# A hybrid trunk on one core: when the first block's mean square is finished, and which projections run on unnormed channels

## The chip, the cores and the metric

The kernel runs on one core of a Trainium2 chip. The engines of a core are TensorE (PE, matrix products; PEld is its weight load), VectorE (DVE), ScalarE (ACT), GpSimd (POOL) and SyncE (SP, which here issues nearly all transfers, one after another, on a queue of its own). Matrix products leave their sums in PSUM; everything else lies in SBUF or in device memory. The metric is the device time of one execution in microseconds (us).

## The reference, cut to what matters

One layer of a streaming encoder: 2048 tokens, 1024 channels. The first half is an RMS norm, one combined projection, three token mixers that read columns of it, and an output projection; the second half is a gated convolutional network.

```
def rms_norm(x, g):
    xf = x.astype(jnp.float32)
    y = xf * lax.rsqrt(jnp.mean(xf * xf, axis=-1, keepdims=True) + RMS_EPS)
    return (y * g.astype(jnp.float32)).astype(x.dtype)
...
def rwkv7_time_mix(u, mu, w0, w2, a0, a2, g2, k_k, k_a, r_k, lnx_g, lnx_b):
...
    u = u + (u_prev - u) * mu
    r, k, v, w_lo, a_lo, g_lo = jnp.split(u, C_SPLITS, axis=-1)
    w = w0 + jnp.tanh(w_lo) @ w2
```

The mixers are A (chunked softmax attention), B (forgetting attention), both with RMS-normed queries and keys per head of 64 channels, and C (an RWKV-7 recurrence). The factor 1/rms of a token is one number for all its 1024 channels, so a projection of the unnormed channels (times the gain g) may be multiplied by that factor afterwards.

## The kernel before, in words

Tokens are worked on in four blocks of 512. Channels lie on the 128 partitions, so that x of a block is 8 tiles of 128 x 512. Products are made in a split form: a value is a high part `hi` and a rest `lo`, and `project` adds hi·hi, hi·lo and lo·hi for each of the 8 tiles, 24 matmuls in all (L281 to L283). The normalised tiles are called hT. The weights of a projection come by `load_w`: a raw load of 0.5 MB on SP's queue (L270, tile `wraw`, two buffers), a cast of the high part on ACT (L160), the subtraction of the low part on DVE (L161), and a store of the split 1 MB for the later blocks (L273, `wD`).

`prepare` makes the factor: squares of the 8 tiles on ACT (L325), their sum on POOL and DVE (L327, L329), a product with ones on PE (L332), Ln and Exp on ACT (L336, L337, result `rsb`), and the normalisation of x on DVE (L341). `block_in` casts the normalised tiles into hT (L160, L161). In the first block two projections (j12 and j13, the inputs of the decay, the learning rate and the gate) take unnormed tiles `hR`, and their sums are multiplied by `rsb` afterwards (L370). The pool of hT and hR has one buffer for each tile, so a normalised tile is written where the unnormed one was read.

```
    hR = [hTp.tile([P, 2, TB], F32R, name=f"hT{kt}") for kt in range(KT)]
...
    weave((), lora_in(hR, lo0, scale))
    for b in range(NB):
        hT = block_in(xs)
```

`qk_in` makes a query or key tile q0 to q7: a projection, its square on ACT (L700), a product with a block matrix on PE (L703), Ln and Exp (L705, L706), a multiplication (L708), a split into `qh` and `ql`, and two stores on SP (L712, L713). In the first block the projections named in `PRE` come first, then k, r and v of the recurrent mixer in `rwkv_front` (L294 to L300 mix a token with the one before it; L394 and L395 are four small products, whose sigmoid is `sigw`, L305; L423 to L447 prepare the chunks; L467 is the first product of the chunks). `rwkv_back` is the recurrence over chunks: PE adds to `z` (L658, L659), and ACT and DVE make the next state S from it (L662, L663).

The order of instructions on each engine is made when the program is built, by a scheduler that goes by priorities: a priority is the place in the written order, and `tc.high_priority(offset=200)` puts what stands in it 200 places ahead. `weave` and `pipelined` interleave jobs by their count of matmuls; `pipelined` parks a job that yields 0 until `PARK` = 3 tiles of the next projection are through.

Of the kernel before, what the change touches and what calls it, by code (L numbers as in the profile page):

```python
# [33 lines left out]
PACE = 1  # L34
KSTAT = 1
X0N = 1
PRE = "q0 q1"
PLAN0 = ["", "q2 q3 q7", "q4 q6 q5 v1", "v0"]
PLAN = ["q1 v0", "q2 q3", "q4 q5 v1", "q6 q0 q7"]
LAST = ["", "", "v0", "q2 q0", "q1 q6 q3", "q4 v1 q5 q7"]  # L40
# [56 lines left out]
def trunk_kernel(ctx: ExitStack, tc: tile.TileContext, xT, w_in, pp, cst, cau, rel, relr, w2, a2, g2, w_out, w_up, w_down, out, dbg=None):  # L97
    nc = tc.nc
# [80 lines left out]
    def t512(name, tag, dt=F32):  # L179
        return (flp if tag == "fl" else t2k).tile([P, TB], dt, name=name, tag=tag, bufs=BUFS[tag])  # L180
# [74 lines left out]

    kept = {}

    def pair(n):
        return wl.tile([P, 2, n, 1040 // n], F32R, name="w", tag="w", bufs=BUFS["w"])

# [15 lines left out]
    def project(hT, c0, raw=None, who="P"):  # L276

        hi, lo = load_w(0, c0, P, KT, raw)
        ps = psm[who].tile([P, TB], F32, name="mm", tag="ps")
        for kt in range(KT):  # L280
            mm(ps, hi[:, kt, 0:P], hT[kt][:, 0, :], start=(kt == 0), stop=False)  # L281
            mm(ps, hi[:, kt, 0:P], hT[kt][:, 1, :], start=False, stop=False)  # L282
            mm(ps, lo[:, kt, 0:P], hT[kt][:, 0, :], start=False, stop=(kt == KT - 1))  # L283
            yield 3
        return ps
# [23 lines left out]
    def prepare(b, xs, rsbs=None):  # L309

        acc = t512("acc", "fl")

        def load(kt):
            if b == 0:
                return x0[kt]
            xt = xtp.tile([P, TB], F32, name="xt", bufs=BUFS["xt"])
            nc.sync.dma_start(out=xt, in_=xT[kt * P : (kt + 1) * P, b * TB : (b + 1) * TB])
            return xt

        accs = [acc, t512("acc", "fl")] if b == 0 else [acc]  # L320
        n = KT // len(accs)
        for kt in range(KT):
            a, first = accs[kt // n], kt % n == 0
            sq = a if first else t512("sq", "fl")
            nc.scalar.activation(sq, load(kt), AF.Square)  # L325
            if not first:
                (nc.vector if kt // n else LEV["acc"](nc)).tensor_tensor(a, a, sq, op=ALU.add)  # L327
        if b == 0:
            nc.vector.tensor_tensor(acc, acc, accs[1], op=ALU.add)  # L329
        yield 12  # L330
        ps = psm["S"].tile([P, TB], F32, name="mm", tag="ps")
        mm(ps, cn("ones"), acc, start=True, stop=True)  # L332
        rsb = xtp.tile([P, TB], F32, name="rsb")
        if rsbs is not None:
            rsbs.append(rsb)
        nc.scalar.activation(rsb, ps, AF.Ln, scale=1.0 / DM, bias=eps[:, 0:1])  # L336
        nc.scalar.activation(rsb, rsb, AF.Exp, scale=-0.5)  # L337

        def normed(kt):
            xt = load(kt)  # L340
            nc.vector.scalar_tensor_tensor(xt, xt, par("mix_g", kt), rsb, op0=ALU.mult, op1=ALU.mult)  # L341
            return xt

        n = BUFS["xt"] if b else KT
        xs.extend([normed(kt) for kt in range(n)] + [functools.partial(normed, kt) for kt in range(n, KT)])
# [12 lines left out]
    def lora_in(hT, res, scale=None):  # L358
        pss = []
        for j in (12, 13):  # L360
            pss.append((yield from project(hT, CB + j * P, raw0 if scale and j == 12 else None)))
            if scale is None:
                lora_out(j, pss[-1], res)
        if scale is not None:
            rsb = scale()

            def scaled():
                for j in (12, 13):
                    t = t512("t", "fl")
                    nc.vector.tensor_tensor(t, pss[j - 12], rsb, op=ALU.mult)  # L370
                    lora_out(j, t, res)

            late.append(scaled)
# [193 lines left out]
            rows = slice(c * 64, c * 64 + 32)  # L567
            copy(e, DT[rows, :, c * 64 + 32 : c * 64 + 64], ps[rows].rearrange("p w s i -> p (w s) i"))

    def urgent():  # L570
        return tc.high_priority(offset=200)

    def rwkv_back(s):

        b, i, lg, KR, DT, LZ, v, bD, EC = (s[n] for n in ("b", "i", "lg", "KR", "DT", "LZ", "v", "bD", "EC"))
# [116 lines left out]
        nc.vector.tensor_tensor(yl, yl, gps, op=ALU.mult)  # L692
        nc.gpsimd.dma_start(out=yD[512 + i * P : 512 + (i + 1) * P, b * TB : (b + 1) * TB], in_=yl)

    def qk_in(b, hT, n):

        ts_ = slice(b * TB, (b + 1) * TB)
        ps = yield from project(hT, (0, 128, 256, 384, 768, 896, 1024, 1152)[n], None, "Q")
        sq = t512("sq", "fl")
        nc.scalar.activation(sq, ps, AF.Square)  # L700
        yield 0
        sps = psm["q"].tile([P, TB], F32, name="mm", tag="ps")
        mm(sps, cn("blk"), sq, start=True, stop=True)  # L703
        rn = t512("rn", "fl")
        nc.scalar.activation(rn, sps, AF.Ln, scale=1.0 / 64, bias=eps[:, 0:1])  # L705
        nc.scalar.activation(rn, rn, AF.Exp, scale=-0.5)  # L706
        g = qkg[:, n // 2 : n // 2 + 1]
        nc.vector.scalar_tensor_tensor(rn, ps, g, rn, op0=ALU.mult, op1=ALU.mult)  # L708
        qh = t512("qh", "fl", F32R)
        ql = t512("ql", "fl", F32R)  # L710
        split(qh, ql, rn, None, LEV['ql'](nc))
        nc.sync.dma_start(out=qkD[n, 0, :, ts_], in_=f(qh))  # L712
        nc.sync.dma_start(out=qkD[n, 1, :, ts_], in_=f(ql))  # L713
# [54 lines left out]
        nc.sync.dma_start(out=ckD[:, 0, ts_], in_=f(ch))  # L768
        nc.sync.dma_start(out=ckD[:, 1, ts_], in_=f(cl))

    def pipelined(jobs):

        parked = None
        for job in jobs:
            k = 0
            for w in job:
                if w == 0:
                    if parked is not None:
                        yield from parked
                    parked = job  # L780
                    break
                yield w
                k += 1
                if parked is not None and k == PARK:
                    yield from parked
                    parked = None
        if parked is not None:
            yield from parked
# [33 lines left out]
        for _ in stream:  # L822
            pass

    def fill(b, hT, names):
        return pipelined([v_in(b, hT, int(n[1])) if n[0] == "v" else qk_in(b, hT, int(n[1])) for n in names.split()])

    plan, last = PLAN, LAST
    def bias_rows():
# [27 lines left out]
    def scale():  # L857
        for _ in prep:
            pass
        return rsb0[0]  # L860

    weave((), lora_in(hR, lo0, scale))
    for b in range(NB):
        hT = block_in(xs)
        xs = []
        jobs = (PLAN0 if b == 0 else plan) if b + 1 < NB else last
        lo = {} if b else lo0
        for i in range(4):
            res = {}
            if b == 0 and i == 0:  # L870
                late.pop()()
                weave((), fill(b, hT, PRE))
            fills[:] = [fill(b, hT, jobs[i])]
            weave(
                (back, inv),
                lora_in(hT, lo) if i == 0 and b else (),
                rwkv_front(b, i, hT, lo, res),
                prepare(b + 1, xs) if i == 2 and b + 1 < NB else (),
                fills[0],
            )  # L880
            back, inv = (rwkv_back(prev) if prev else None), rwkv_inverse(res)
            prev = res
            if b == 1 and i == 1:
                bias_rows()
            if b == 2 and i == 0:
                bias(0, nc.sync)
# [593 lines left out]
```

## Time and profile before

| | us |
|---|---|
| median of three runs | 3197.59 |
| lowest and highest of them | 3186.72, 3198.84 |
| the profiled execution, its own time | 3200.97 |
| its span | 3199.2 |
| PE busy | 3007.5 |

The rows further down are of that execution. Times are counted from the start of its span. A timeline's row says when an instruction (or a group of equal ones, x2) started, how long it took, the engine, the line and the tile, and in brackets how long the engine had been idle and what ended that. A matmul's length is modelled, so the step from one to the next says more than the length shown. The mean granted clock of PE over the span was 0.967 of full speed.

### The profile page before, as it was taken

To read this page: it belongs to the slowest core of one execution; us is meant where nothing else is said; L and a number is where in the kernel's file an instruction comes from. 1 tells how busy PE (TensorE), PEld (TensorE's weight loads), DVE (VectorE), ACT (ScalarE), POOL (GpSimd) and SP (SyncE) were. 2 spreads that over 40 slices of the span, in tenths; PEclk is the share of its full clock that TensorE was granted. 3 is DMA by queue.
4 is the path that set the end of the run, shared out by engine and by line. 5 is a ranking of instruction groups with operands and counts; after the bars stand their busy time and mean duration, and the time that the engine had idled before them with its cause. 6 is when DMAs were issued, how large, how long until landed. Compare 5 with 4: busy or idle time off the path is not lost.

```text
span 3199.2 us, 49138 instructions
## 1 busy us (share of the span) xinstructions
PE 3007.5 (94%) x17820; PEld 2634.3 (82%) x17820; DVE 2366.6 (74%) x4590; ACT 1398.1 (44%) x2610; POOL 955.5 (30%) x928
## 2 busy tenths in 40 slices
PE   6988999999999989999989899998999998999999
PEld 4666777777777756667789899998999998899998
DVE  6667676756777646777462888889988888888886
ACT  5444444544443335678532433434333434333332
POOL 1010010001001021144241444444444445444443
PEclk8988999999999979999999999999999999999999
DMA  7756665655644475423234322222422222422221
GB/s 223 210 166 182 194 176 150 175 158 166 187 122 128 134 177 152 132 77 94 67 118 133 132 80 80 80 79 79 147 80 80 80 80 84 136 75 76 80 80 68
DMA packets 310818, 392.92 MB, mean 123 GB/s; under 512 B 137144, under 2 KB 228804, under 8 KB 299752
## 3 DMA queue, kind: packets, MB, share of 16 engines
q1 hardware_dynamic: 305936, 378.44, 40.3%
q0 software_dynamic: 2816, 8.39, 0.9%
q10 hardware_dynamic: 1824, 2.95, 0.4%
q8 instruction: 141, 2.31, 0.3%
q14 instruction: 101, 0.83, 0.1%
HBM read 304.65 MB, written 86.36 MB: 122 GB/s over the span
## 4 chain that ended last, share of the span: by engine, by line
PE 66%; DVE 17%; DMA 5%; issue 5%; ACT 4%; POOL 2%; SPq 1%; POOLq 0%; ACTq 0%; DVEq 0%
PE ps L1307 7%; PE ps L1306 7%; PE ps L1305 7%; PE ps L1351 4%; PE ps L1353 4%; PE ps L1352 4%; PE mm L283 2%; PE mm L281 2%; PE mm L282 2%; PE o L1077 2%; PE z L658 2%; DVE T L536 2%; DVE tm L533 2%; PE ps L1213 2%; DVE wu L161 2%
## 5 line engine op out<-in xcount | busy, mean ns | idle before, releaser
L1307 PE MATMUL ps<-B,wu 128*128 128x340 f32 (+1 forms) x1848 | 593.9, 321 | 19.7 <-DVE wu L161 19.6
L1305 PE MATMUL ps<-B,wu 128*128 128x340 f32 (+1 forms) x1848 | 590.1, 319 | 3.0 <-ACT wu L160 2.1
L1306 PE MATMUL ps<-B,wu 128*128 128x340 f32 (+1 forms) x1848 | 590.7, 320 | 0.0
L1307 PEld LDWEIGHTS ps<-B,wu 128*128 128x128 f32 x1848 | 349.1, 189 | 26.8 <-DVE wu L161 26.4
L1351 PE MATMUL ps<-hid,wd 128*128 128x340 f32 (+1 forms) x1056 | 341.2, 323 | 13.9 <-ACT wd L160 10.3
L1305 PEld LDWEIGHTS ps<-B,wu 128*128 128x128 f32 x1848 | 349.0, 189 | 3.6 <-ACT wu L160 2.4
L1306 PEld LDWEIGHTS ps<-B,wu 128*128 128x128 f32 x1848 | 348.2, 188 | 0.1
L1353 PE MATMUL ps<-hid,wd 128*128 128x340 f32 (+1 forms) x1056 | 337.2, 320 | 4.5 <-POOL wd L161 4.5
L1352 PE MATMUL ps<-hid,wd 128*128 128x340 f32 (+1 forms) x1056 | 339.0, 321 | 0.0
L281 PE MATMUL mm<-hT,w 128*128 128x512 f32 x704 | 314.6, 447 | 20.8 <-ACT w L160 13.6
L161 DVE TENSOR_TENSOR wu<-S,wu 128x512 fp32r<-128x512 f32 x264 | 255.9, 976 | 74.9 <-ACT wu L160 74.9
L282 PE MATMUL mm<-hT,w 128*128 128x512 f32 x704 | 289.3, 411 | 6.8 <-DVE hT L161 6.1
L283 PE MATMUL mm<-hT,w 128*128 128x512 f32 x704 | 289.6, 411 | 1.9 <-DVE w L161 1.8
L1354 DVE TENSOR_TENSOR acc<-acc,ps 128x340 f32<-128x340 f32 (+1 forms) x528 | 247.4, 503 | 48.8 <-PE ps L1353 48.7
L161 POOL TENSOR_TENSOR wd<-raw,wd 128x1024 fp32r<-128x1024 f32 x66 | 171.7, 2621 | 271.5 <-ACT wd L160 271.4
L160 ACT CAST wu<-S 128x512 fp32r<-128x512 f32 x264 | 162.9, 618 | 150.3 <-PE ps L1307 144.1
L1351 PEld LDWEIGHTS ps<-hid,wd 128*128 128x128 f32 x1056 | 200.8, 190 | 17.3 <-ACT wd L160 11.1
L161 DVE TENSOR_TENSOR wu<-raw,wu 128x512 fp32r<-128x512 f32 x198 | 202.6, 1024 | 5.5 <-ACT wu L160 5.5
L1353 PEld LDWEIGHTS ps<-hid,wd 128*128 128x128 f32 x1056 | 200.4, 190 | 6.7 <-POOL wd L161 6.7
L1352 PEld LDWEIGHTS ps<-hid,wd 128*128 128x128 f32 x1056 | 200.9, 190 | 0.0
L160 ACT CAST wu<-raw 128x512 fp32r<-128x512 f32 x198 | 121.0, 620 | 165.7 <-PE ps L1307 145.8
L281 PEld LDWEIGHTS mm<-hT,w 128*128 128x128 f32 x704 | 138.4, 197 | 63.1 <-ACT w L160 14.8
(337 smaller groups left out, 6811.6 us busy)
## 6 DMA issues: line engine op xcount, KB each, us to landing
w<-wD SPq DMA_DIRECT2D x72, 1024.0 KB, 6.8
raw<-in_w_up_dram SPq DMA_DIRECT2D x132, 512.0 KB, 3.6
raw<-in_w_down_dram SPq DMA_DIRECT2D x66, 512.0 KB, 3.5
wD<-w SPq DMA_DIRECT2D x24, 1024.0 KB, 5.5
wraw<-in_w_in_dram SPq DMA_DIRECT2D x24, 512.0 KB, 6.2
xt<-in_xT_dram SPq DMA_DIRECT2D x48, 256.0 KB, 4.8
K<-qkD SPq DMA_DIRECT2D x21, 512.0 KB, 8.1
Q<-qkD SPq DMA_DIRECT2D x84, 128.0 KB, 3.0
```

Source lines behind the costliest of these rows:

```text
L160: (hi_eng or nc.scalar).copy(hi, src) if (hi_eng or nc.scalar) is nc.scalar else hi_eng.tensor_copy(out=hi, in_=src)
L161: (lo_eng or nc.vector).tensor_tensor(lo, src, f(hi), op=ALU.subtract)
L281: mm(ps, hi[:, kt, 0:P], hT[kt][:, 0, :], start=(kt == 0), stop=False)
L282: mm(ps, hi[:, kt, 0:P], hT[kt][:, 1, :], start=False, stop=False)
L283: mm(ps, lo[:, kt, 0:P], hT[kt][:, 0, :], start=False, stop=(kt == KT - 1))
L1305: mm(ps, whl[:, 0, kt, :], Bs[p][:, kt, 0, 0:n], start=(kt == 0), stop=False)
L1306: mm(ps, whl[:, 0, kt, :], Bs[p][:, kt, 1, 0:n], start=False, stop=False)
L1307: mm(ps, whl[:, 1, kt, :], Bs[p][:, kt, 0, 0:n], start=False, stop=(kt == 3))
L1351: mm(ps, wd[:, 0, ch], hid[:, 0, cs], start=(u == 0), stop=False)
L1352: mm(ps, wd[:, 0, ch], hid[:, 1, cs], start=False, stop=False)
L1353: mm(ps, wd[:, 1, ch], hid[:, 0, cs], start=False, stop=(u == G - 1))
L1354: nc.vector.tensor_tensor(acc[ct][:, cs], acc[ct][:, cs], ps, op=ALU.add)
```

## The change

Three things. q0 leaves `PRE` and becomes a third projection on the unnormed tiles, followed by a multiplication of its sum by `rsb`, before its square. The rest of `prepare` (ones-product, Ln, Exp, normalisation) is written between j12 and j13 instead of behind both. And the squares of `prepare`, their additions, and the square in `qk_in` stand under `tc.high_priority(offset=200)`; this holds for all blocks.

```
-PRE = "q0 q1"
+PRE = "q1"
...
-            nc.scalar.activation(sq, load(kt), AF.Square)
-            if not first:
-                (nc.vector if kt // n else LEV["acc"](nc)).tensor_tensor(a, a, sq, op=ALU.add)
+            xt = load(kt)
+            with urgent():
+                nc.scalar.activation(sq, xt, AF.Square)
+                if not first:
+                    (nc.vector if kt // n else LEV["acc"](nc)).tensor_tensor(a, a, sq, op=ALU.add)
...
+            elif j == 12:
+                rsb = scale()
         if scale is not None:
-            rsb = scale()
...
-    def qk_in(b, hT, n):
+    def qk_in(b, hT, n, rsb=None):
...
+        if rsb is not None:
+            yield 0
+            t = t512("t", "fl")
+            nc.vector.tensor_tensor(t, ps, rsb, op=ALU.mult)
+            ps = t
         sq = t512("sq", "fl")
-        nc.scalar.activation(sq, ps, AF.Square)
-        yield 0
+        with urgent():
+            nc.scalar.activation(sq, ps, AF.Square)
+        if rsb is None:
+            yield 0
...
+    first = qk_in(0, hR, 0, rsb0[0])
+    while next(first):
+        pass
...
-                weave((), fill(b, hT, PRE))
+                weave((), fill(b, hT, PRE, first))
```

`fill` and `pipelined` take the started q0 as a job that is already parked. Lines of the changed kernel carry other numbers (L332 is L337 there, L341 is L346, L658 is L661, L467 is L473).

On PE the program counts 16340 instructions in both kernels, on DVE one more. The order differs up to about the end of the first tenth of the span and is the same from there. It differs most at three places.

At the start, on DVE, the sum of squares is followed in the kernel before by the low weights of j13 and of q0 (one row, x2), and then by the eight normalisations, the first three of which are shown:

```order
L329 TENSOR_TENSOR acc<-acc 128x512
L161 TENSOR_TENSOR w<-wraw,w 128x8x128 x2
L341 SCALAR_TENSOR_TENSOR x_123<-x_123,pps,rsb 128x512
L341 SCALAR_TENSOR_TENSOR x_124<-x_124,pps,rsb 128x512
L341 SCALAR_TENSOR_TENSOR x_125<-x_125,pps,rsb 128x512
```

In the changed kernel the eight normalisations (the last three are shown) stand ahead of the same low weights, and the multiplication of j12's sum follows them:

```order
L346 SCALAR_TENSOR_TENSOR x_128<-x_128,pps,rsb 128x512
L346 SCALAR_TENSOR_TENSOR x_129<-x_129,pps,rsb 128x512
L346 SCALAR_TENSOR_TENSOR x_130<-x_130,pps,rsb 128x512
L161 TENSOR_TENSOR w<-wraw,w 128x8x128 x2
L376 TENSOR_TENSOR t<-mm,rsb 128x512
```

So the low weights moved from ahead of the normalisations to behind them. On PE the ones-product moved from behind j13 to ahead of it; in the changed kernel it follows j12's last tile (hT_202), and two matmuls each of j13 and q0 on the first unnormed tile (hT_195) follow it, before the first that reads low weights (L286):

```order
L286 MATMUL mm<-hT_202,w 128x512
L337 MATMUL mm<-acc,csts 128x512
L284 MATMUL mm<-hT_195,w 128x512
L285 MATMUL mm<-hT_195,w 128x512
L284 MATMUL mm<-hT_195,w 128x512
L285 MATMUL mm<-hT_195,w 128x512
L286 MATMUL mm<-hT_195,w 128x512
```

On SP's queue, between the first weight stores and the weights of r and v, the kernel before has the stores of q1's and k's split weights (wD_128, wD_2052), the raw loads of r's and v's weights, and then q0's two stores (the first pair of qkD):

```order
L273 DMA wD_128_410<-w 2048x1x128
L273 DMA wD_2052_468<-w 2048x1x128
L270 DMA wraw<-in_w_in_dram 128x8x128 x2
L712 DMA qkD<-qh 128x512
L713 DMA qkD<-ql 128x512
```

The changed kernel has q0's stores first:

```order
L276 DMA wD_128_408<-w 2048x1x128
L276 DMA wD_2052_470<-w 2048x1x128
L722 DMA qkD<-qh 128x512
L723 DMA qkD<-ql 128x512
L273 DMA wraw<-in_w_in_dram 128x8x128 x2
```

So the two raw loads moved past two stores. On ACT, too, the casts of these two weights moved: they stood on either side of q1's square, and now stand behind it and behind q1's Ln, Exp and cast, directly ahead of the mix of k and the sigmoid `sigw`.

The third place is on PE in the first block, behind the square product of the third group of heads (L427, L433), at about 158 us of the profile. The kernel before has six matmuls of a projection (on hT_317 and others) between two steps of the recurrence:

```order
L427 MATMUL mm<-sq,cst_143 128x512
L281 MATMUL mm<-hT_317,w 128x512
L282 MATMUL mm<-hT_317,w 128x512
L283 MATMUL mm<-hT_317,w 128x512
L658 MATMUL z<-UV,LZ 128x64 x2
L659 MATMUL z<-S_187,QA 128x128
L281 MATMUL mm<-hT_320,w 128x512
L282 MATMUL mm<-hT_320,w 128x512
```

In the changed kernel four steps follow each other, and the projection (on hT_349) begins behind them:

```order
L433 MATMUL mm<-sq,cst_143 128x512
L661 MATMUL z<-UV,LZ 128x64 x2
L662 MATMUL z<-S_187,QA 128x128
L661 MATMUL z<-UV,LZ 128x64 x2
L662 MATMUL z<-S_187,QA 128x128
L661 MATMUL z<-UV,LZ 128x64 x2
L662 MATMUL z<-S_187,QA 128x128
L661 MATMUL z<-UV,LZ 128x64 x2
L662 MATMUL z<-S_187,QA 128x128
L661 MATMUL z<-UV,LZ 128x64
L284 MATMUL mm<-hT_349,w 128x512
```

So the matmuls that lay between the steps moved behind them, towards the ones-product of the second block.

## Rows read from the trace of the kernel before

**Rows 1.** The page: the span, and busy time and share of each engine.

```profile
span 3199.2 us, 49138 instructions
...
PE 3007.5 (94%) x17820; PEld 2634.3 (82%) x17820; DVE 2366.6 (74%) x4590; ACT 1398.1 (44%) x2610; POOL 955.5 (30%) x928
```

**Rows 2.** The page: shares by engine of the chain that ended last.

```profile
PE 66%; DVE 17%; DMA 5%; issue 5%; ACT 4%; POOL 2%; SPq 1%; POOLq 0%; ACTq 0%; DVEq 0%
```

**Rows 3.** Windows: length, busy PE, PEld, DVE, ACT, POOL, clock, DMA share, GB/s.

```profile
0.00:85.00 85.00, 57.91 (x196) 40.88 (x196) 54.55 (x94) 48.96 (x74) 11.33 (x20) 0.86 0.79 230
38.00:43.00 5.00, 4.97 (x12) 3.91 (x13) 5.00 (x9) 1.51 (x3) 0.00 (x0) 0.50 0.00 0
303.00:320.00 17.00, 10.35 (x39) 8.61 (x39) 10.43 (x32) 4.78 (x12) 0.00 (x0) 0.51 0.70 198
```

**Rows 4.** Timeline of PE: start, length, what, and the idle time before it.

```profile
20.28 0.79 PE L281 MATMUL mm<-hT,w 128*128 128x512 f32 x1 [2.84 <-ACT w L160]
...
29.55 1.02 PE L332 MATMUL mm<-acc,csts 128*128 128x512 f32 x2
...
38.03 0.79 PE L282 MATMUL mm<-hT,w 128*128 128x512 f32 x1 [4.01 <-DVE hT L161]
...
44.08 0.39 PE L281 MATMUL mm<-hT,w 128*128 128x512 f32 x1
...
57.48 1.97 PE L703 MATMUL mm<-sq,cst 128*128 128x512 f32 x2 [4.73 <-ACT sq L700]
...
65.65 0.40 PE L394 MATMUL mm<-lw,w2s 128*128 128x512 f32 x1
...
67.26 0.51 PE L281 MATMUL mm<-hT,w 128*128 128x512 f32 x1
...
72.92 1.02 PE L427 MATMUL mm<-sq,cst 128*128 128x512 f32 x2
...
83.03 2.08 PE L467 MATMUL rw<-KR,AK 64*128 64x128 f32 x16 [3.54 <-DVE v L297]
```

**Rows 5.** Timeline of ACT.

```profile
6.54 1.05 ACT L160 CAST w<-wraw 128x1024 fp32r<-128x1024 f32 x1 [0.39 <-DMA wraw<-in_w_in_dram]
...
55.89 1.04 ACT L160 CAST w<-wraw 128x1024 fp32r<-128x1024 f32 x1 [1.01 <-DMA wraw<-in_w_in_dram]
...
57.60 1.05 ACT L160 CAST w<-wraw 128x1024 fp32r<-128x1024 f32 x1 [0.17 <-DMA wraw<-in_w_in_dram]
...
66.51 0.69 ACT L305 ACTIVATE sigw<-mm,nwa 128x512 f32<-128x512 f32 x1
...
72.01 1.05 ACT L160 CAST w<-wraw 128x1024 fp32r<-128x1024 f32 x1 [0.29 <-DMA wraw<-in_w_in_dram]
```

**Rows 6.** Timeline of DVE.

```profile
20.32 0.69 DVE L329 TENSOR_TENSOR acc<-acc 128x512 f32<-128x512 f32 x1
...
31.99 5.39 DVE L341 SCALAR_TENSOR_TENSOR x<-x,pps,rsb 128x512 f32<-128x512 f32 x8 [8.71 <-ACT rsb L337]
...
76.29 1.22 DVE L161 TENSOR_TENSOR w<-wraw,w 128x1024 fp32r<-128x1024 f32 x1
```

**Rows 7.** Timeline of SP's queue: the issue of transfers.

```profile
1.65 0.43 SPq L188 DMA_DIRECT2D wraw<-in_w_in_dram  x1
...
47.20 5.42 SPq L270 DMA_DIRECT2D wraw<-in_w_in_dram  x2
...
65.54 2.35 SPq L270 DMA_DIRECT2D wraw<-in_w_in_dram  x2
```

**Rows 8.** Timelines of ACT and PE at the second block's ones-product.

```profile
190.73 0.61 ACT L325 ACTIVATE sq<-xt 128x512 f32<-128x512 f32 x1
...
192.86 2.08 PE L332 MATMUL mm<-acc,csts 128*128 128x512 f32 x2 [4.68 <-POOL acc L327]
```

**Rows 9.** Timeline of PE at two steps of the recurrence.

```profile
166.07 0.66 PE L658 MATMUL z<-UV,LZ 128*128 128x64 f32 x4 [0.49 <-DVE S L663]
...
303.41 1.12 PE L658 MATMUL z<-UV,LZ 128*128 128x64 f32 x4 [0.91 <-DVE S L663]
```

More of the change, by code (lines that the diff above doesn't have):

```diff
@@ L256, in trunk_kernel, with urgent @@
     kept = {}
+    def urgent():
+        return tc.high_priority(offset=200)
     def pair(n):
@@ L568, in rwkv_inverse @@
             copy(e, DT[rows, :, c * 64 + 32 : c * 64 + 64], ps[rows].rearrange("p w s i -> p (w s) i"))
-    def urgent():
-        return tc.high_priority(offset=200)
     def rwkv_back(s):
@@ L769, in forget, with pipelined @@
         nc.sync.dma_start(out=ckD[:, 1, ts_], in_=f(cl))
-    def pipelined(jobs):
-        parked = None
+    def pipelined(jobs, parked=None):
         for job in jobs:
@@ L823, in weave, with fill @@
             pass
-    def fill(b, hT, names):
-        return pipelined([v_in(b, hT, int(n[1])) if n[0] == "v" else qk_in(b, hT, int(n[1])) for n in names.split()])
+    def fill(b, hT, names, parked=None):
+        return pipelined([v_in(b, hT, int(n[1])) if n[0] == "v" else qk_in(b, hT, int(n[1])) for n in names.split()], parked)
     plan, last = PLAN, LAST
```

## The prediction, made before the changed kernel ran

> **What bounds the kernel now.** I read the page first. TensorE (PE) is busy 94% of a span of 3199.2 us [rows 1], and the chain that ended last is 66% PE and 17% DVE [rows 2]. So a microsecond off PE's gaps, or off the work that PE does at its low clock, is worth about a microsecond, and a microsecond off an engine beside it is worth nothing by itself. The view by windows then says where PE is not full: in the first 85 us it is busy 57.91 us at a mean granted clock of 0.86 [rows 3], and the change begins there.
>
> PE's timeline of that stretch gives the places [rows 4]. The second lora projection starts at 20.28. The ones-product of the mean square starts at 29.55. PE then waits for normalised channels, is back at 38.03, and runs projections q0 and q1 until 57.48 − 4.73 = 52.75. It waits 4.73 us for q1's square, runs k up to 65.65, r from 67.26, and waits again, 3.54 us, for DVE before 83.03. After each wait of 2.84 us or more PE is slow. In 38 to 43 the clock is 0.50, the 1.2 GHz level [rows 3]. From 38.03 to 44.08 there are 14 matmuls, 6.05 / 14 = 0.43 us each; r's 24 take 72.92 − 67.26 = 5.66 us, 0.236 each, at the 2.4 GHz level. I use these two prices throughout: 24 matmuls cost 5.7 us at the high clock, and 14 × 0.43 + 10 × 0.236 = 8.4 us after a long wait.
>
> **The change part by part.** The listed order is the same on every engine after about 0.3 ms, so everything lies in the first tenth of the span; the rest moves by what the start gains or loses.
>
> *The early product.* DVE ends the sum of squares at 20.32 + 0.69 = 21.0 [rows 6], and the product may follow at once. From the product's start to the first normalisation it took 31.99 − 29.55 = 2.44 us (product, Ln, Exp). So the factor is there at about 23.5 instead of 31.99, 8.5 us sooner. What becomes of it is decided by DVE's order: the eight normalisations (5.39 us, [rows 6]) now stand before the low weights of j13 (about 1.2 us, the length of one such instruction at 76.29). PE can do only four matmuls without those weights, so its bulk starts at 23.5 + 5.4 + 1.2 = 30.1, at the low clock. 44 matmuls (j13's and q0's) follow: 14 × 0.43 + 30 × 0.236 = 13.1, to 43.2. Before, q0 was through with 24 matmuls from its start, at 46.2 (44.08 and nine more at 0.236). **3.0 us sooner.**
>
> *q1.* Its normalised tiles lie in the buffers of the unnormed ones, and the last is free only when q0 ends. The last cast (a tile half as wide as the weight tile that takes 1.04 at 55.89 [rows 5]: 0.6, an estimate), the weight cast (1.04) and the low weights (1.2) follow: about 46. q1's raw weights are issued behind the low weights of j13 and q0, at about 30.1 + 1.2 = 31.3, and even at 55.89 − 47.20 = 8.7 us [rows 5, 7] they land at 40, so this load is hidden by some 3 us. PE waited 2.8 us and is slow: 46 + 8.4 and a square product (0.5) give 55.0. **2.2 us later than 52.75**: this eats most of the first gain.
>
> *The urgent square.* Before, q1's square stood behind the cast of r's weights, which itself waited for a load [rows 5]. Now the square comes first: one ACT pass, some 0.75 us of wait, instead of 4.73, and the clock should hold. The product (two passes of 0.236) and k's 24 matmuls: 55.0 + 0.75 + 0.47 + 5.66 = 61.9, against 65.65. **3.8 us sooner.**
>
> *What the square has been moved past.* The raw loads of r's and v's weights now stand behind q0's two stores on SP's queue (the order in the section on the change). Those wait for q0's square product, which ends at 46 + 9 × 0.43 + 0.6 = 50.5, and then for Ln, Exp, multiplication, cast and subtraction one after another on ACT and DVE, 0.7 each as in [rows 5, 6] and with hand-overs some 4 us: stores at 54.5, and with two issues of 0.7 (an estimate, above the 0.43 at 1.65 [rows 7]) the loads at about 55.9 instead of 47.20. Landing took 6.54 − 1.65 = 4.9 us on an empty queue, 8.7 us behind two 1 MB stores (47.20), and 72.01 − 65.54 = 6.5 us behind two small stores like these [rows 5, 7]. I take 6.4 (the cast starts just after the landing), the nearest. The second load was 57.60 − 55.89 = 1.7 us behind the first. On ACT both casts now stand ahead of the mix of k and of the decay's sigmoid, and r's projection waits for the latter, since it reads the PSUM tile that r needs: 55.9 + 6.4 + 1.7 = 64.0, cast 1.04, mix and sigmoid 0.69 each (66.51 in [rows 5]): r starts at 66.4, against 67.26. But PE has then stood from 61.9 + 1.6 (four small products, 65.65 to 67.26) = 63.5, 2.9 us, and the row at 20.28 says that after 2.84 us the clock is low: r takes 8.4 instead of 5.7 and ends at 74.8, against 72.92. On DVE a second low-weights instruction stands between r and the product at 83.03, +1.2. So that product goes to 83.03 + 1.9 + 1.2 ≈ 86.1, **3.1 us later**; with the clock held, 0.4 later. Landing at 4.9 makes r start at 64.9 with a wait of 1.4: r ends at 70.6 and the product comes 1 us sooner. Landing at 8.7 gives 5.4 later. I take +3, bounds −1 and +5.5.
>
> By the Trainium skill, "DMA: Bandwidth & Descriptors", section "Anatomy of one DMA — SWDGE (gpsimd) path", a transfer costs about 2.0 us plus its bytes at 436 GB/s, so 0.5 MB would land some 3.2 us after issue; the section is on the software path, while this queue is SP's. No row here of this load is that short (4.9 at the least), so the rows decide; by the page the second load would land at about 61.8, r would start near 64.2 at the high clock, and this term would be about −1.6.
>
> The one new instruction, q0's multiplication, is 0.7 us on DVE beside PE's 8.4 us of q1, ahead of nothing that ends last there: nothing, or 0.7 without that cover.
>
> *The second ones-product.* At 192.86 PE waits 4.68 us for block 1's squares, the last of them behind the group norm on ACT (190.73) [rows 8]. Now all eight squares are urgent and their loads stand ahead of stores. The wait should go, and the slow spell behind it (up to 14 matmuls at 0.2 extra): about −7. Paid for it: four steps of the recurrence (L658, now L661) stand back to back where v's projection used to lie between them. With cover a step waits 0.49 at most [rows 9]; bare it waited about 0.9 (303.41), at a clock of 0.51 in that window [rows 3, 9]. Four waits of 1.0, less the old 0.5, are 3.5; if v then starts slow, 14 × 0.2 = 2.8 more, 6.3. So the term is −3.5 to −0.7; I take **−2**, since between these ends the row at 303.41 is nearest to the slow one. Its bounds are −5 (steps as covered as before) and +1.
>
> *The rest of 200 to 300 us* is rearranged without a visible new wait: 0, ±4.
>
> **Sum**: +3 − 2 + 0 = +1. The profiled run took 3200.97, 3.4 above the median of the three; 3202 there is 3198.6 against a median of 3197.59. I predict 3198. A measurement of this kernel tells about 0.5% (16 us) from no change; its three runs lie 12.1 us apart.
>
> **The rivals.**
> 1. *Slower: the weights of r land late.* If they need 8.7 us, as behind the stores at 47.20, r starts at 68.7 and the product after it is 5.4 later; with v slow after bare steps the second place gives only −0.7. About +5, up to +10 if the next raw loads, behind two stores now, are late as well. For it: two 1 MB stores are issued some 6 us ahead; against it: the load at 65.54, behind stores as small as q0's, took 6.5. It decides from a landing of about 7 us.
> 2. *Faster: r never slows.* Landing at 4.9, r at 64.9 at the high clock (−1), and the second ones-product for −4 to −7: −5 to −8. For it: a lone square ahead of q1's product; against it: two of the three loads shown took over 6 us. The skill's figure above would make it so too, −1.6 − 4 ≈ −5.6.
> 3. *The change does not do what it says:* the early factor and the urgent squares shift work, but DVE's chains (from 67 to 83, and through the recurrence) set the times as before; each place within 1 us, total within ±2 and the same time as now. Against it: the waits of 4.73 and 4.68 are plainly not DVE's.
> 4. *The rearranged 200 to 300 us* costs or gives 8 to 16 through a wait that the order does not show.
>
> **How the numbers follow.** Forecast (net −3 to +4): 0.40. Rival 1 (+4 to +10): 0.20. Rival 2 (−4 to −11): 0.22. Rival 3: 0.10. Rival 4: 0.08, half each way. The range takes in rivals 1 and 2 and leaves out rival 4: 3198 − 12 = 3186 to 3198 + 10 = 3208. The forecast's own range is 3194 to 3202. Beyond 0.5% (below 3181.6, above 3213.6) lies only rival 4's end and what I overlooked: 0.04 faster, 0.04 slower, 0.92 the same.
>
> **What would show it.** The ones-product at 21 to 22 us and the first normalisation near 23.5; the bulk of j13 from about 30; q0 ending near 43; q1 from 46 at half clock, with a wait of under 1 us for its square product in place of 4.73; r near 66 behind a wait of about 3, its matmuls at 0.43; the first L473 near 86 in place of 83.03. At 190 to 200, no wait of 4.7 before the ones-product, and four waits of about 1 us near 160 to 170. The prediction is wrong if r's weights land well under 5 us or over 8, if the normalisations do not hold up the low weights, or if the orders from 200 to 300 meet a wait of their own.

## The result, and the profile after

The changed kernel is slower: the median of seven runs is 3219.38 us (3205.23 to 3226.02), that of the kernel before over seven runs 3198.84 (3186.72 to 3200.89). The ratio on record is 1.0062, with a 95% interval of 1.0046 to 1.0078. The forecast was 3198, with a range that ended at 3208; both the number and the range were missed.

The first thing to see is the page of the changed kernel, its span and its first row of engines:

```profile
span 3203.5 us, 49122 instructions
...
PE 3009.7 (94%) x17820; PEld 2631.2 (82%) x17820; DVE 2371.1 (74%) x4591; ACT 1397.5 (44%) x2610; POOL 948.4 (30%) x928
```

Beside [rows 1] it tells nearly nothing. This profiled execution (3205.23 us) was also the quickest of the seven. A loss of 20 us in 3200 has to be looked for by place, and the way that worked was to set the two timelines side by side at instructions that both kernels have. The square product of the recurrent mixer (L427 before, L433 now) is such a mark: it comes once for each group of heads. In the kernel before it starts at 72.92 [rows 4], and then, by the timeline of PE, among others at

```profile
261.19 0.59 PE L427 MATMUL mm<-sq,cst 128*128 128x512 f32 x1
...
346.28 0.59 PE L427 MATMUL mm<-sq,cst 128*128 128x512 f32 x1
```

(the front section gave the one between them as "about 158 us"; it starts at 157.70). In the changed kernel the same marks stand at

```profile
72.26 0.59 PE L433 MATMUL mm<-sq,cst 128*128 128x512 f32 x1
...
159.32 0.59 PE L433 MATMUL mm<-sq,cst 128*128 128x512 f32 x1
...
268.04 0.59 PE L433 MATMUL mm<-sq,cst 128*128 128x512 f32 x1
...
360.02 0.59 PE L433 MATMUL mm<-sq,cst 128*128 128x512 f32 x1
```

The shift at these four marks is −0.7, +1.6, +6.9 and +13.7 us. So the start, where the change was made, costs almost nothing, and 12 us are lost from 158 to 346 us of the old time, where nothing was changed in the code but the priority of the squares. (The mark comes five times up to there; the one at 102.28, now 104.39, is left out, its shift is +2.1.)

The view by windows, cut at these marks, says what the 12 us are. Columns as in [rows 3]: length, busy PE and the other engines, then PE's clock. First the kernel before, in the two stages and in a fixed stretch inside them:

```profile
157.70:261.20 103.50, 87.80 (x490) 68.76 (x489) 73.12 (x209) 46.13 (x94) 12.04 (x15) 0.88 0.62 180
261.20:346.30 85.10, 74.07 (x442) 59.96 (x441) 58.19 (x162) 38.99 (x79) 4.69 (x14) 0.88 0.61 170
198.00:230.00 32.00, 29.69 (x222) 24.07 (x221) 12.59 (x27) 12.27 (x26) 2.76 (x7) 1.00 0.64 197
```

Then the changed kernel, in its first 85 us and in the same stages:

```profile
0.00:85.00 85.00, 58.51 (x188) 39.27 (x190) 54.09 (x94) 48.17 (x73) 10.70 (x20) 0.86 0.74 218
159.30:268.00 108.70, 91.93 (x483) 70.90 (x482) 72.40 (x196) 46.48 (x93) 13.10 (x15) 0.83 0.62 174
268.00:360.00 92.00, 80.36 (x447) 65.50 (x447) 60.24 (x176) 40.02 (x81) 4.73 (x14) 0.81 0.57 159
198.00:230.00 32.00, 26.46 (x136) 20.33 (x134) 11.56 (x24) 12.87 (x26) 2.73 (x7) 0.78 0.68 187
```

The two stages together are 200.7 us long in place of 188.6, 12.1 more. PE is busy 172.29 of them in place of 161.87, 10.4 more, for the same matmuls (between the first and the last of these marks both timelines hold 928, of the same kinds); it is idle 28.4 in place of 26.7, only 1.7 more. Busy longer with the same matmuls is a lower clock: 0.83 and 0.81 in place of 0.88 and 0.88. A mean clock c over a length t stands for 2 × (1 − c) × t microseconds at the 1.2 GHz level: 37 + 35 = 72 us now, 25 + 20 = 45 before. 27 us more at half speed are 13 us of work not done, near the 10.4 that the busy time shows.

The start looks as follows on PE's timeline, for [rows 4]:

```profile
20.79 1.12 PE L337 MATMUL mm<-acc,csts 128*128 128x512 f32 x2
24.29 0.79 PE L284 MATMUL mm<-hT,w 128*128 128x512 f32 x1 [2.38 <-ACT w L160]
29.91 0.80 PE L286 MATMUL mm<-hT,w 128*128 128x512 f32 x1 [3.45 <-DVE w L161]
...
44.70 0.80 PE L284 MATMUL mm<-hT,w 128*128 128x512 f32 x1 [2.31 <-ACT w L160]
...
55.58 1.12 PE L713 MATMUL mm<-sq,cst 128*128 128x512 f32 x2 [0.69 <-ACT sq L709]
...
62.12 0.40 PE L400 MATMUL mm<-lw,w2s 128*128 128x512 f32 x1
...
65.05 0.80 PE L284 MATMUL mm<-hT,w 128*128 128x512 f32 x1 [1.25 <-ACT sigw L308]
...
68.56 0.40 PE L286 MATMUL mm<-hT,w 128*128 128x512 f32 x1
...
84.16 2.08 PE L473 MATMUL rw<-KR,AK 64*128 64x128 f32 x16 [5.32 <-DVE AK L453]
```

These are the forecast's stations: the product at 20.79, the bulk of j13 held up for low weights until 29.91, q0 done at 44.70 − 2.31 = 42.39, q1's square product after a wait of 0.69 in place of 4.73, k done at 62.12, r at 65.05, and the first product of the chunks at 84.16, which was at 83.03 before.

### The profile page after: what moved, and what is told of

Its sections match the earlier page's. It is cut to its first block, busy times and chain, and to the rows that moved or that the text cites. A ratio compares the mean times of both kernels' runs of the same rounds, so it can differ in the third digit from the quotient of the medians.

```text
span 3203.5 us, 49122 instructions
## 1 busy us (share of the span) xinstructions
PE 3009.7 (94%) x17820; PEld 2631.2 (82%) x17820; DVE 2371.1 (74%) x4591; ACT 1397.5 (44%) x2610; POOL 948.4 (30%) x928
## 3 DMA queue, kind: packets, MB, share of 16 engines
q8 instruction: 141, 2.31, 0.3%
## 4 chain that ended last, share of the span: by engine, by line
PE 54%; DVE 8%; issue 4%; DMA 2%; ACT 2%; POOL 2%; SPq 0%; POOLq 0%; ACTq 0%; DVEq 0%
PE ps L1319 7%; PE ps L1318 7%; PE ps L1317 7%; PE ps L1365 4%; PE ps L1363 4%; PE ps L1364 4%; PE o L1089 2%; PE ps L1225 2%; PE ps L1226 2%; PE ps L1224 1%; PE st L1071 1%; PE st L1072 1%; DVE B L161 1%; DVE wu L161 1%; PE s L1033 1%
## 5 line engine op out<-in xcount | busy, mean ns | idle before, releaser
L286 PE MATMUL mm<-hT,w 128*128 128x512 f32 x704 | 289.7, 412 | 5.5 <-DVE w L161 5.4
L1365 PEld LDWEIGHTS ps<-hid,wd 128*128 128x128 f32 x1056 | 200.7, 190 | 6.5 <-POOL wd L161 6.5
```

Source lines behind the costliest of these rows:

```text
L1365: mm(ps, wd[:, 1, ch], hid[:, 0, cs], start=False, stop=(u == G - 1))
```

## The experiments

Twelve kernels, three batches of four, each timed in five rounds against the kernel before on its chip. The diffs are against the kernel that the sentence names. Two theories ran through most of them. Theory A: the order that the scheduler made behind the early product costs the time. Theory B: the start itself does, through r's late weights. Theories C and D belong to one experiment and are told in its expectation. The order of a run is compared by its trace, from the first chunk product on, by line and tile.

**The changed kernel again**, for a second profile.

> The changed kernel once more, for a second profile. Theory A (the rearranged order from 150 to 350 us costs the time, and what follows only passes it on): about 3219 again, ratio 1.006, the shift against the kernel before about +2 us at 150 us of the profile, +13 at 345, and this time not given back behind 460 us. Theory B (the start is what costs, through r's late weights): a shift of 10 us or more already at 85 us.

Measured: 3220.39 us, ratio 1.006 [1.0042, 1.0079]. The shift at the first chunk product is +0.9, at the four marks −0.9, +1.4, +6.4 and +13.4. Theory A's picture repeats to half a microsecond. The time behind the fourth mark does not: in the first profile the shift fell from 14 to 4.3 us by the end of the span, in this one it rose to 21.

**The product late, the rest as changed** (against the changed kernel):

```
-            elif j == 12:
-                rsb = scale()
         if scale is not None:
+            rsb = scale()
```

> The third unnormed projection and the urgent squares stay; the ones-product goes back behind j13. With that the order on PE from 85 us on is nearly that of the kernel before. Theory A: the loss goes, ratio 0.997 to 1.001 (3190 to 3202), no growth of the shift from 150 to 350 us. Theory B, or a theory that the third projection or the urgent squares cost it: still 1.004 or more.

Measured: 3196.24 us, ratio 0.9985 [0.9966, 1.0005]. The loss is gone. The order on PE behind 85 us is again that of the kernel before, the two stages take 186.8 us, and the start is 7.4 us ahead. "Late" holds for the written order alone: on PE the ones-product still runs at 21.46 us, since the priority of its squares brings it there (the run with that priority alone, further down, shows the same).

**The priority alone** (against the kernel before; the same lines for the square in `qk_in`):

```
-            nc.scalar.activation(sq, load(kt), AF.Square)
-            if not first:
+            xt = load(kt)
+            with urgent():
+                nc.scalar.activation(sq, xt, AF.Square)
+                if not first:
```

> Only the raised priority of the squares, on the kernel before. The order on PE differs from before in few places. Theory A: same, 0.998 to 1.001, and the wait of 4.7 us for q1's square falls under 1 us, which brings 3 to 5 us by 66 us of the profile. A theory that the priority itself costs (squares ahead of other ACT work): 1.003 or more.

Measured: 3190.63 us, ratio 0.9969 [0.995, 0.9988]: faster than the kernel before and the changed one. But not as expected: q1's wait is still 4.57 us. The 7.8 us at the first chunk product come from elsewhere, which the last batch settles.

**The early product alone** (against the kernel before):

```
+            elif j == 12:
+                rsb = scale()
         if scale is not None:
-            rsb = scale()
```

> Only the early ones-product, with q0 on normed channels and ordinary priority. It moves the order on PE from 85 us on about as much as the full change. Theory A: slower, 1.003 to 1.008, with the shift growing between 150 and 350 us. Theory B: 0.998 to 1.002, as r's weights are not held up by q0's stores more than before.

Measured: 3231.22 us, ratio 1.009 [1.0065, 1.0116], the slowest of all, with a start that is 3.3 us ahead. Its windows at the marks:

```profile
153.40:272.80 119.40, 99.98 (x516) 79.33 (x515) 77.80 (x216) 48.86 (x101) 13.82 (x15) 0.81 0.62 179
272.80:363.90 91.10, 78.11 (x423) 63.10 (x422) 55.02 (x162) 36.80 (x72) 4.67 (x14) 0.79 0.57 162
```

210.5 us in place of 188.6, and 45 + 38 = 84 us at the low level (rounded after adding). The direction is theory A's, the ratio lies above the 1.003 to 1.008 expected. The loss is there without the third projection and without any priority. One part of the expectation was wrong: q0's stores do stand ahead of the loads of r's and v's weights here (stores from 50.50 and 52.90 on SP's queue, loads from 54.12 and 57.40). Theory B falls by the start itself, which is ahead and not late.

**The full change without the priority** (against the changed kernel: both `with urgent():` around squares taken out).

> The full change with ordinary priority for the squares. Its order on PE is that of the changed kernel but for two instructions. If the order after the early product is the cause and the priority gives 10 us of its own, as the run with the priority alone suggests: 3222 to 3234, ratio 1.007 to 1.011. If the priority only works together with the late product: 3215 to 3223, like the full change.

Measured: 3214.71 us, ratio 1.005 [1.003, 1.0069]. Neither branch: without the priority this order is, if anything, a little faster, so the 10 us that the priority brings alone are not to be had with the early product. The two stages take 197.6 us where the changed kernel takes 200.7, although only two instructions stand elsewhere on PE (the second profile of the changed kernel repeats its stages to 0.2 us): some 3 us hang on more than PE's order.

**The value weights on another queue.** At 213 to 229 us the changed kernel runs the chunk products bare, without matmuls of a projection between them, and the raw load of the weights for those matmuls stands at 219.24 on SP's queue (218.61 in the second profile). The edit (against the changed kernel, and as a control on the kernel before) issues these loads from GpSimd:

```
-                nc.sync.dma_start(out=raw[:, :, 0:w], in_=w_in[...])
+                (nc.gpsimd if w > P else nc.sync).dma_start(out=raw[:, :, 0:w], in_=w_in[...])
```

> The changed kernel with the raw loads of the attention values' weights (the 256 and 260 columns wide ones) issued by GpSimd, on its own queue, in place of SP's. In the changed kernel the one of them that the matmuls at 229 us need is issued at 218.6, behind the chunk inverses' transfers. Theory C (PE runs the chunk products at about 213 to 229 us bare, since the matmuls that filled them wait for these weights): the loads are early, the matmuls stand in the chunk products again, and 5 to 12 us come back by 300 us of the profile; ratio to the kernel before 1.001 to 1.004. Theory D (the place of this load does not matter, the slow clock and the recurrence's own waits do): 1.005 to 1.008 as without it.

> The same move of these loads on the kernel before, as the control: there one of the two is issued at 191.8 us already. Theory C: little to win, 0.997 to 1.001, less than on the changed kernel. Theory D or a general gain by a second queue: as much won here as on the changed kernel.

Measured: 3221.3 us, ratio 1.0069 [1.0043, 1.0095], and for the control 3209.35, 1.0023 [1.0007, 1.004]. Theory C fell, the ratio is the one of theory D. The matmuls did come ahead of these chunk products and between them, and there the clock is high (0.96 from 198 to 230 in place of 0.78), but the loss came up elsewhere, at recurrence steps that now stand bare: 204.1 us for the two stages.

```profile
198.00:230.00 32.00, 29.62 (x198) 25.27 (x198) 13.78 (x26) 12.58 (x26) 4.32 (x9) 0.96 0.82 250
240.00:265.00 25.00, 17.11 (x72) 13.36 (x72) 18.19 (x54) 14.53 (x31) 0.75 (x1) 0.64 0.45 124
```

The control came out by neither branch, and says more than it was made for: the kernel before, moved to a new order by an edit that only changes the queue of these loads, lost 8 us too, in the same stages (197.2 us).

**The third projection alone** (against the kernel before: the change without the early product and the priority).

> Only the third unnormed projection: product late, ordinary priority. Order on PE from 85 us on as before. From the runs with it and the urgent squares (0.9985) and with these squares alone (0.9969): 1.000 to 1.003. If the third projection is what gains and the priority costs in its company: under 0.998.

Measured: 3201.94 us, ratio 1.0 [0.9983, 1.0016]. The order on PE behind 85 us and the stages (189.0 us) are as before.

**The product early, the normalisations late** (against the changed kernel):

```
         nc.scalar.activation(rsb, rsb, AF.Exp, scale=-0.5)
+        if rsbs is not None:
+            yield 0
...
             elif j == 12:
-                rsb = scale()
+                next(prep)
         if scale is not None:
+            rsb = scale()
```

> The changed kernel, with its product early and its eight normalisations given out only behind j13: the factor comes as early, the low weights of j13 stand behind two normalisations in place of eight, and one of the two raw loads of r's and v's weights stands ahead of q0's stores. From 85 us on its order on PE is that of the changed kernel but for 16 instructions. If the order from 160 to 350 us costs the time whatever the start does: the shift at 85 us is 3 to 6 us better than the changed kernel's, but it grows by 10 to 14 us again; 3211 to 3219, ratio 1.003 to 1.006. If the blocked start is behind all of it: 1.001 or less.

Measured: 3213.99 us, ratio 1.0038 [1.0022, 1.0055]. This is the run that parts start and order. The first chunk product is 5.1 us ahead of before, the first mark 7.9 ahead, since j13's low weights wait for two normalisations only; and from the second mark to the fourth the shift goes from −4.0 to +7.1, by 11.1 us, as in the changed kernel. Its windows:

```profile
153.70:261.30 107.60, 89.50 (x484) 68.60 (x483) 72.12 (x196) 46.37 (x93) 13.11 (x15) 0.86 0.63 178
261.30:353.30 92.00, 80.36 (x447) 65.51 (x446) 60.20 (x175) 39.92 (x80) 4.73 (x14) 0.81 0.56 159
```

The second row is the changed kernel's second stage to the microsecond (92.00, 80.36, 0.81).

**The priority of the mean square alone** (against the kernel before: the diff of the priority alone, without the line in `qk_in`).

> The priority on the squares of the mean square and their sums alone, on the kernel before. If these bring the gain (the product earlier without a moved order): 0.996 to 0.999, a shift of -5 to -9 us at 85 us. If the query square brings it: 0.999 to 1.001.

Measured: 3191.43 us, ratio 0.9966 [0.9951, 0.9981]. All of the gain is here. Rows of its PE timeline in the start, and its windows:

```profile
21.60 0.59 PE L338 MATMUL mm<-acc,csts 128*128 128x512 f32 x1
```

```profile
149.70:250.40 100.70, 84.35 (x489) 65.58 (x488) 72.62 (x209) 46.40 (x94) 11.96 (x15) 0.92 0.65 186
250.40:335.50 85.10, 73.78 (x441) 59.72 (x441) 57.93 (x162) 38.90 (x79) 4.97 (x14) 0.88 0.61 169
```

With the squares first on ACT the scheduler itself puts the ones-product at 21.60, 8 us ahead of [rows 4], with the code where it was; the start gains 8.3 us, and since the order on PE behind stays, they are kept.

**Another offset** (against the changed kernel):

```
-        return tc.high_priority(offset=200)
+        return tc.high_priority(offset=300)
```

> The changed kernel with an offset of 300 in place of 200 for what is urgent: another order from 85 us on, 250 entries from the changed kernel's and 540 from before's. If the slow clock in 158 to 346 us is what costs, the time follows the microseconds at half clock there: about half of what they exceed the 44 us of the kernel before, whichever way that falls; an order nearer to the changed kernel's gives 1.003 to 1.008. If it is the start alone: 1.005 to 1.007 as the changed kernel, whatever the clock there.

Measured: 3217.98 us, ratio 1.0042 [1.0024, 1.006]. Start +0.3 us, stages 200.7 us, 69 us at the low level. By the expectation half of 69 − 45, 12 us, should be lost in the stages; 12.1 were, 3.4 of them idle time. The ratio alone does not part the two branches: its interval holds most of both.

**The priority of the query square alone** (against the kernel before).

> The priority on the query square alone, on the kernel before. If q1's square ahead of the weight cast brings 3 to 4 us as forecast: 0.998 to 0.9995 and a wait under 1 us for its product; if the product waits as long as before, 0.9995 to 1.001.

Measured: 3200.33 us, ratio 0.9997 [0.998, 1.0013]; the product waits even longer than before:

```profile
57.91 1.22 PE L706 MATMUL mm<-sq,cst 128*128 128x512 f32 x1 [6.04 <-ACT sq L703]
```

Taken together, from the profile of each kernel (start: shift at the first chunk product; stages: the two from mark to mark; low: from their two clocks as above):

| kernel | start | stages | PE idle | low | ratio |
|---|---|---|---|---|---|
| before | 0 | 188.6 | 26.7 | 45 | 1 |
| third projection alone | −1.6 | 189.0 | 27.4 | 45 | 1.0 |
| query square's priority | +0.6 | 188.7 | 26.8 | 43 | 0.9997 |
| mean square's priority | −8.3 | 185.8 | 27.7 | 37 | 0.9966 |
| both priorities | −7.8 | 185.5 | 27.0 | 36 | 0.9969 |
| change, product written late | −7.4 | 186.8 | 28.3 | 37 | 0.9985 |
| before, other queue | −0.7 | 197.2 | 30.0 | 59 | 1.0023 |
| early product, late normalisations | −5.1 | 199.6 | 29.7 | 65 | 1.0038 |
| offset 300 | +0.3 | 200.7 | 30.1 | 69 | 1.0042 |
| change, no priority | +1.5 | 197.6 | 30.5 | 59 | 1.005 |
| the change | +1.1 | 200.7 | 28.4 | 72 | 1.0062 |
| change, other queue | +1.1 | 204.1 | 36.0 | 64 | 1.0069 |
| early product alone | −3.3 | 210.5 | 32.4 | 84 | 1.009 |

The upper six have, from the first chunk product on, the order on PE of the kernel before; the lower seven have moved orders. Start and stages together give the ratio's order but for neighbours, and the low microseconds part the two groups without overlap (at most 45 above, at least 59 below). In each lower row the excess idle time plus half of the excess low time comes to 1.7 to 3.3 us more than the excess of the stages over 188.6 (the change: 1.7 + 13.5 = 15.2 against 12.1), so this count is somewhat high and gets the order right.

## Why the prediction was wrong

*What bounds the kernel* held: PE, and what PE does at its low clock. The steps of the start held as well, in part by luck. The product, j13's bulk and q0's end were forecast at 21 to 22, 30.1 and 43.2, and came at 20.79, 29.91 and 42.4; q1 was through at 55.58 − 0.69 = 54.9 (55.0), k at 62.12 (61.9). r's weights landed sooner than taken: their cast starts at 61.10 behind an issue at 55.27, 5.8 us in place of 6.4, so r began at 65.05, not 66.4. The first chunk product came 1.1 us late where 3 were taken, within the bounds of −1 and +5.5. The Trainium skill's cost of a transfer ("DMA: Bandwidth & Descriptors", "Anatomy of one DMA — SWDGE (gpsimd) path"), fitted on GpSimd's path and not on SP's, gives an estimate of 3.2 us for this landing; the 5.8 here side with the rows. (The prediction's sentence on that figure has a slip: 55.9 + 3.2 + 1.7 is 60.8 for the second load, not 61.8; the forecast does not use it.)

Two things in the start were not as taken. q1 began at 44.70 where 46 was taken and needed 10.2 us where 8.9 were, so that its end at 54.9 is two misses that cancel. And r waited 1.25 us only, which by the prediction should have left the clock high ("Landing at 4.9", a wait of 1.4 and 5.7 us for r); yet its first eight matmuls took (68.56 − 65.05) / 8 = 0.44 us each, the price of the low clock, and r took 7.2 us. So already here a wait near 1 us went with the low clock, as the price by waits alone did not allow for.

*The urgent square* was right in size and wrong in its reason. The wait fell from 4.73 to 0.69. But the priority of the query square alone leaves it at 6.04, and the full change without any priority has the same 0.69:

```profile
54.17 1.13 PE L711 MATMUL mm<-sq,cst 128*128 128x512 f32 x2 [0.69 <-ACT sq L707]
```

Nor does it take the cast of r's weights to make the product wait: with both priorities on the kernel before, the square stands ahead of that cast, and the product still waits 4.57 us.

```profile
47.77 0.59 ACT L704 ACTIVATE sq<-mm 128x512 f32<-128x512 f32 x1
...
48.41 2.08 PE L707 MATMUL mm<-sq,cst 128*128 128x512 f32 x2 [4.57 <-ACT sq L704]
...
48.87 1.05 ACT L160 CAST w<-wraw 128x1024 fp32r<-128x1024 f32 x1 [0.51 <-DMA wraw<-in_w_in_dram]
```

ACT works there from 38.64 to 47.77 without a pause that shows, on q0's chain and on the inputs of the decay and the gate. In the changed kernel the work on these inputs is through at 47.38 + 0.61 = 47.99, and ACT waits 0.84 us for PE before the square:

```profile
54.93 0.60 ACT L709 ACTIVATE sq<-mm 128x512 f32<-128x512 f32 x1 [0.84 <-PE mm L286]
```

And the priority that did bring time, that of the mean square's squares, was given no price in the start; alone it makes the product come at 21.60 without moving code, worth 8 us there.

*The second ones-product*: its wait did go (L337 runs at 195.95 with none shown), and four bare steps took its place, with waits of 0.73, 1.09, 0.73 and 2.66 us:

```profile
161.73 0.66 PE L661 MATMUL z<-UV,LZ 128*128 128x64 f32 x4 [0.73 <-DVE S L666]
...
163.76 0.88 PE L661 MATMUL z<-UV,LZ 128*128 128x64 f32 x4 [1.09 <-DVE S L666]
...
165.90 1.11 PE L661 MATMUL z<-UV,LZ 128*128 128x64 f32 x4 [0.73 <-DVE S L666]
...
170.20 0.66 PE L661 MATMUL z<-UV,LZ 128*128 128x64 f32 x2 [2.66 <-DVE Y L157]
```

From 157.70 to the next square product of a query (198.12 before, 200.46 now) the net is +0.7 us, where −2 was taken with bounds of −5 and +1.

*The step that failed* is the one-line term **"The rest of 200 to 300 us is rearranged without a visible new wait: 0, ±4"**. It measured +11.4: the shift is +2.3 at 198 us and +13.7 at 346. It was looked at for waits, and there are hardly any (1.7 us of idle time). What the new order does is take the projections' matmuls out from between the small products of the chunks. PE's timeline of the changed kernel, at 213 to 227 us, shows it:

```profile
213.76 1.08 PE L564 MATMUL rw<-D,NO 128*128 128x32 f32 x8 [2.37 <-DVE D L560]
215.52 1.97 PE L571 MATMUL rw<-E,BP 128*128 128x64 f32 x8 [0.68 <-DVE BP L157]
...
222.54 0.47 PE L589 MATMUL rw<-csts,v 128*128 128x128 f32 x1 [1.22 <-ACT R L595]
...
224.87 1.97 PE L604 MATMUL rw<-UV,LZ 64*64 64x64 f32 x32 [1.22 <-ACT R L595]
```

Each wait is short and none would stand out in a list of waits, but the clock over 198 to 230 is 0.78, and 136 matmuls are done in these 32 us where 222 were at a clock of 1.00. Up to the mark at 268 this is 4.5 of the 11.4 us. The second stage loses the larger part, 6.9, in the same way. In the kernel before, matmuls with the values' weights stand between the chunk products of 287.94 and 294.92, and what follows bare lasts to the projection at 320.8. In the changed kernel these matmuls are through at 300.63, and what follows bare, now with more of the chunk products in it, lasts to 334.1. Two rows of each timeline, then the windows of the two bare stretches, the kernel before first:

```profile
287.94 0.27 PE L587 MATMUL rw<-csts,KR 128*128 128x128 f32 x1
...
294.92 1.15 PE L601 MATMUL rw<-UV,LZ 64*64 64x64 f32 x32
...
300.63 0.60 PE L687 MATMUL rw<-csts,Y 128*128 128x128 f32 x4
...
305.86 0.68 PE L604 MATMUL rw<-UV,LZ 64*64 64x64 f32 x16 [1.22 <-ACT R L595]
...
294.90:320.80 25.90, 17.87 (x129) 14.78 (x129) 17.26 (x49) 8.31 (x20) 0.00 (x0) 0.66 0.66 183
300.60:334.10 33.50, 24.56 (x145) 19.82 (x143) 17.06 (x47) 11.56 (x28) 1.85 (x2) 0.60 0.55 152
```

So the term alone, +11.4, fits the size of the fourth rival, "costs or gives 8 to 16 through a wait that the order does not show", at a chance of 0.08 shared between the signs; but it came by another mechanism than the rival named, the clock and not a wait, and the whole loss of 20 us lies beyond it. Its term should have been bounded by the clock: [rows 3] already show 17 us at 0.51 in this stretch, so a new order could bring more or less of that.

What is shown: that the order which the scheduler makes when the product's code is moved up, and no other part of the change, loses the time (the change with the late product loses nothing, though its product runs at 21.46; the early product alone loses most; with a start 8 us better at the first mark and nearly the same order the same 11 us are lost again). What is read from rows and not tested by itself: that the bare small products are what holds the clock low. The run with the other queue for the value weights speaks for it, since there the chunk products with matmuls between them ran at the high clock; but no kernel filled them with the order kept. What stays open: how a loss of 13.7 us at 360 us becomes 19 to 20 at the end. Behind that point the order is the same, and two profiles of the same kernel went from 14 to 4 and from 13 to 21, so single executions scatter there by ±10 us.

## What to carry to other kernels

Where a scheduler makes the order, price an edit by the whole new order, stage by stage, and not by the lines that moved: look at what stands between small dependent products, and ask of each place at which clock it will run. A raised priority that moved an existing step by 8 us with the rest of the order unchanged was worth 0.34%; moving the code for the same 8 us changed the order of the next 260 us and lost 0.9% alone, 0.6% with the rest of the change. The version to keep is the kernel before with the priority on the mean square's squares alone, 3191.43 us, ratio 0.9966 [0.9951, 0.9981].

## What was not expected of the hardware

The loss shows in busy time and hardly in waits: in two stages of 200 us PE's idle time rose by 1.7 us and its busy time, for the same matmuls, by 10.4, at a granted clock of 0.83 and 0.81 in place of 0.88. That the short waits between small products bring the low clock is the reading given above, not a test.

And an order that differs by a small edit can cost as much as a real delay: the value weights' loads on a second queue took the kernel before from 45 to 59 us at the low level and made it 0.23% slower. Whether the queue itself has a part in this is open: the wait before the second block's ones-product is 6.51 us there in place of 4.68, but the 8 us are lost behind the mark at 259.91, in the second stage alone (93.2 us in place of 85.1).
